# Five small early writes on the store queue, spaced by Pool fills, ahead of a split SiLU-and-multiply kernel

## The chip, the cores and the metric

The kernel runs on one core of one Trainium2 chip. The metric is device time in microseconds (us), the median of several executions. The kernel does no TensorE work. ACT (ScalarE) and DVE (VectorE) compute, Pool (GpSimd) fills, and SP (SyncE) issues DMAs; L74 is line 74 of the kernel.

## The reference, cut to what matters

```python
batch, seq, dim = (32, 512, 2048)          # x, float32
half_dim = x.shape[-1] // 2
x1, x2 = x[..., :half_dim], x[..., half_dim:]
silu_x1 = x1 * (1 / (1 + np.exp(-x1)))
return (silu_x1 * x2).astype(np.float32)   # (32, 512, 1024)
```

The input has 134.22 MB and the output 67.11 MB. There is little arithmetic per byte.

## The kernel before

The 16384 rows are cut into 16 tiles of 128 partitions x 8 rows. Loads are issued from ACT's queue and stores from SP's queue. Two input buffers and two output buffers rotate.

```python
    in_pool = ctx.enter_context(tc.tile_pool(name="in_pool", bufs=2))
    out_pool = ctx.enter_context(tc.tile_pool(name="out_pool", bufs=2))
    # ... cut ...
    def load(i):
        xt = in_pool.tile([P, K, in_cols], dt, name="xt")
        nc.scalar.dma_start(out=xt[:, :plan[i][1], :], in_=view(x_flat, i))
        loaded[i] = xt

    load(0)
    load(1)
    for i in range(n_tiles):
        # ... cut ...
        ot = out_pool.tile([P, K, half], dt, name="ot")
        for c in range(0, k, KC):                      # KC = 2: four pieces
            # ... cut: ACT writes silu into ot, DVE multiplies ot by the other half of xt ...
            if last:
                nc.sync.dma_start(out=ov[:, c:ce, :], in_=ot[:, c:ce, :])
        if not last:
            nc.sync.dma_start(out=ov, in_=ot[:, :k, :])
        if i + 2 < n_tiles:
            load(i + 2)
```

Load i+2 is issued only when tile i has been multiplied, because it reuses that tile's input buffer. Tile i can start only when the output buffer of tile i-2 has been stored.

Of the kernel before, what the change touches and what calls it, by code (L numbers as in the profile page):

```python
# [1 line left out]

# [4 lines left out]


def issue_ahead_of_the_first_barrier(nc):




    head, body = nc.main_func.blocks[:2]
    load = next(ins for ins in body.instructions if type(ins).__name__ == "InstDMACopy")
    at = next(
        j for j, ins in enumerate(head.instructions)
        if ins.engine == load.engine and type(ins).__name__ == "InstDrain"
    )
    body.instructions = [ins for ins in body.instructions if ins.name != load.name]  # L20
    head.instructions = head.instructions[:at] + [load] + head.instructions[at:]


@with_exitstack
def kernel(
    ctx: ExitStack,
    tc: tile.TileContext,
    x: bass.AP,
    out: bass.AP,
):  # L30






    nc = tc.nc
    P = nc.NUM_PARTITIONS

    x_flat = x.flatten_outer_dims()  # L40
    out_flat = out.flatten_outer_dims()
    num_rows, in_cols = x_flat.shape
    half = in_cols // 2
    dt = x_flat.dtype

    K = 8
    KC = 2
    PLAN = [K] * (num_rows // (P * K))

    in_pool = ctx.enter_context(tc.tile_pool(name="in_pool", bufs=2))  # L50
    out_pool = ctx.enter_context(tc.tile_pool(name="out_pool", bufs=2))

    plan = []
    row = 0
    for k in PLAN:
        plan.append((row, k))
        row += P * k
    assert row == num_rows
    n_tiles = len(plan)

    def view(flat, i):
        row0, k = plan[i]
        return flat[row0:row0 + P * k].rearrange("(p k) d -> p k d", k=k)

    nc.at_finalize(issue_ahead_of_the_first_barrier)


    ctx.enter_context(tc.manual_schedule())

    loaded = {}  # L70
# [5 lines that stand above are left out]

    load(0)
    load(1)
    for i in range(n_tiles):
        k = plan[i][1]  # L80
        xt = loaded.pop(i)
        last = i == n_tiles - 1
        ov = view(out_flat, i)
        ot = out_pool.tile([P, K, half], dt, name="ot")
        for c in range(0, k, KC):
            ce = min(c + KC, k)
            nc.scalar.activation(  # L87
                out=ot[:, c:ce, :],
                in_=xt[:, c:ce, :half],
                func=mybir.ActivationFunctionType.Silu,  # L90
            )
            nc.vector.tensor_mul(  # L92
                out=ot[:, c:ce, :],
                in0=ot[:, c:ce, :],
                in1=xt[:, c:ce, half:],
# [9 lines that stand above are left out]
# [1 line left out]
_INS = ['x']  # L106
_OUTS = [((32, 512, 1024), 'float32')]


# [23 lines left out]
```

## Time and profile before

| | before |
|---|---|
| time, median of 3 runs | 471.02 us (470.53 to 471.09) |
| span of the profiled run | 468.9 us |
| DVE, ACT busy | 30%, 25% |
| load and store packets, share of 16 DMA engines | 66.4% + 33.2% |

Lines of the page of the kernel before: the span, the busy times, the row of slices for DMA (each digit is the busy share of one fortieth of the span, 9 meaning 90% or more), and the two DMA queues with packets, MB and share of 16 engines' span. Queue 10 carries the loads, queue 1 the stores.

```profile
span 468.9 us, 269 instructions
DVE 142.3 (30%) x64; ACT 118.2 (25%) x65; POOL 0.2 (0%) x4
DMA  9899999999999998999999999999999989999998
...
q10 hardware_dynamic: 2304, 134.22, 66.4%
q1 hardware_dynamic: 2736, 67.11, 33.2%
...
out_dram<-ot SPq DMA_DIRECT2D x15, 4096.0 KB, 39.8
```

The two shares add up to 99.6%: the sixteen DMA engines are the limit, from start to end. The other engines wait for data. Any change of the time must show up as DMA work that was added, or as time in which the DMA engines had nothing to do.

The timeline of the kernel before, around the first store (start, duration, engine and line, operation; in brackets the idle time of the engine before it and what ended it):

```profile
32.74 81.08 SPq L100 DMA_DIRECT2D out_dram<-ot  x4
32.75 0.35 ACTq L74 DMA_DIRECT2D xt<-in_x_dram  x1
44.54 7.31 ACT L87 ACTIVATE ot<-xt 128x2048 f32<-128x2048 f32 x4 [15.36 <-DMA xt<-in_x_dram]
46.48 8.89 DVE L92 TENSOR_TENSOR ot<-ot,xt 128x2048 f32<-128x2048 f32 x4 [13.77 <-ACT ot L87]
55.41 0.37 ACTq L74 DMA_DIRECT2D xt<-in_x_dram  x1
```

Store 0 and load 2 are issued at 32.74 us, tile 1 starts at 44.54 us, when its data has landed, and load 3 is issued at 55.41 us. (The SPq line joins the first four stores; only its start is used.)

The trace also has every DMA packet. A load packet is the eight rows of one partition, 64 KB, and takes 2.418 us; a store packet is 32 KB and takes 1.213 us. Here is one engine around the first store of the kernel before, worked out from those records (start in us, L for load or S for store, duration in ns). The records do not name the engine: a packet is put behind the one that ends where it starts. Each DMA also ends, on each engine, with a semaphore packet of 4 bytes (9 ns), which reports its completion; these are left out here:

```
33.27 L 2441   35.72 L 3380   39.09 S 1213   40.30 L 2418   42.71 S 1213   43.91 S 1213   45.10 L 2418
```

On every engine the last load packet before the first store packet is long. The mean excess over 2.42 us is 0.87 us. After that, loads and stores follow each other without a gap and at full speed. The first load packets of the run are long too, by 0.6 us. An intent to make the store queue "warm" can only aim at this 0.87 us, which is 0.2% of the time.

### The profile page before, as it was taken

The page shows a single profiled execution, that of the slowest core. Times are in us where ns is not written, and L with a number is a line of the kernel's source. Part 1 is how long each engine was busy: PE and PEld are TensorE (multiplying, and loading weights), DVE is VectorE, ACT ScalarE, POOL GpSimd, SP SyncE. Part 2 cuts the span into 40 slices and gives each one's busy share as a digit, 9 for nine tenths or more (in the row PEclk, how much of TensorE's full clock was granted, in tenths as well). Part 3 has the DMA queues.
Part 4 walks back from the last instruction along what each step waited for, and adds up shares of the span by engine and source line. Part 5 has one row for each costly group of instructions (what it writes and reads, how often), then busy time and mean ns, then how long its engine had stood idle before and what let it go on. Part 6 is the DMA issues. An engine that isn't in the chain of part 4 may idle for free.

```text
span 468.9 us, 269 instructions
## 1 busy us (share of the span) xinstructions
DVE 142.3 (30%) x64; ACT 118.2 (25%) x65; POOL 0.2 (0%) x4
## 2 busy tenths in 40 slices
DVE  0070705106061160601507025070250702407034
ACT  1142406023060330603206032060420604106051
POOL 0000000000000000000000000000000000000000
DMA  9899999999999998999999999999999989999998
GB/s 431 375 447 403 447 447 447 403 419 431 447 447 403 447 492 363 442 492 391 458 403 439 456 447 403 409 442 447 447 403 444 467 386 447 442 419 481 400 409 354
DMA packets 5042, 201.35 MB, mean 429 GB/s; under 512 B 560, under 2 KB 560, under 8 KB 560
## 3 DMA queue, kind: packets, MB, share of 16 engines
q10 hardware_dynamic: 2304, 134.22, 66.4%
q1 hardware_dynamic: 2736, 67.11, 33.2%
q14 instruction: 2, 0.02, 0.0%
HBM read 134.22 MB, written 67.11 MB: 429 GB/s over the span
## 4 chain that ended last, share of the span: by engine, by line
DMA 80%; DVE 15%; ACT 3%; DVEq 0%; issue 0%
DMA xt<-in_x_dram 80%; DVE ot L92 15%; ACT ot L87 3%; DVEq L128 0%
## 5 line engine op out<-in xcount | busy, mean ns | idle before, releaser
L92 DVE TENSOR_TENSOR ot<-ot,xt 128x2048 f32<-128x2048 f32 x64 | 142.3, 2286 | 319.5 <-ACT ot L87 319.5
L87 ACT ACTIVATE ot<-xt 128x2048 f32<-128x2048 f32 x64 | 116.9, 1897 | 338.8 <-DMA xt<-in_x_dram 338.8
L87 ACT ACT_TABLE_LOAD x1 | 1.3, 1283 | 1.3 <-PEq L117 1.3
L117 POOL MEMSET const-uint8-127<- 128x1 uint8 x1 | 0.1, 102 | 0.0
L117 POOL MEMSET const-bfloat16-1.0<- 128x1 bf16 x1 | 0.1, 101 | 0.0
L117 POOL MEMSET const-float32-0.0<- 128x1 f32 x1 | 0.1, 98 | 0.2 <-issue 0.2
L117 POOL MEMSET const-float32-1.0<- 128x1 f32 x1 | 0.1, 98 | 0.0
## 6 DMA issues: line engine op xcount, KB each, us to landing
out_dram<-ot SPq DMA_DIRECT2D x15, 4096.0 KB, 39.8
out_dram<-ot SPq DMA_DIRECT2D x4, 1024.0 KB, 5.7
xt<-in_x_dram ACTq DMA_DIRECT2D x16, 47.1
```

Of the source, the lines that this page charges most:

```text
L87: nc.scalar.activation(out=ot[:, c:ce, :], in_=xt[:, c:ce, :half], func=mybir.ActivationFunctionType.Silu,)
L92: nc.vector.tensor_mul(out=ot[:, c:ce, :], in0=ot[:, c:ce, :], in1=xt[:, c:ce, half:],)
L117: nc = _bacc.Bacc("TRN2", target_bir_lowering=False, num_devices=1)
```

## The change

The intent, as its form suggests, is to let the store queue do a few tiny writes while the first two loads run, so that its first real store does not pay a start-up cost. Each write sends 512 bytes from each of 16 partitions, one packet per DMA engine, to places that the store of tile 0 overwrites. A Pool fill between the writes spaces them.

```diff
     K = 8
     KC = 2
+    WARM = 5
 ...
     load(0)
     load(1)
+    wt = out_pool.tile([P, K, half], dt, name="ot")
+    for _ in range(WARM):
+        nc.gpsimd.memset(wt[:, :4, :], 0.0)
+        nc.sync.dma_start(out=view(out_flat, 0)[:16, 0, :128], in_=wt[:16, 0, :128])
```

Each fill must wait for the write before it, which reads the tile. The writes stand ahead of store 0 on SP, and store 0 overwrites their bytes. The tile is one of the two output buffers, so tile 1 cannot start before the last small write has landed.

## The prediction

> **What bounds the kernel.** DMA, nearly without a gap. In the page's table of DMA queues the load queue's packets take 66.4% and the store queue's 33.2% of 16 engines' span; in the rows of slices DMA is at 9 throughout, DVE 30%, ACT 25%. In the trace's DMA packets a 64 KB load packet takes 2.418 us, a 32 KB store packet 1.213 us. One engine carries 128 of each: 464.8 of the 468.9 us span. The rest is 1.1 us before the first packet, 0.6 us by which the first load packets are long, 0.87 us per engine by which the last load packet before the first store packet is long (about 3.3 us, starting near 36 us), and 1.2 us after the last. The chain of waits puts 80% on the loads' DMA; its DVE and ACT pieces (15%, 3%) run while DMA is full.
>
> **What the change does.**
> 1. Removes nothing. If the 0.87 us is a cold cost of the store queue (the only candidate for a gain, 0.2%), the first small write now meets it, on engines equally saturated by loads: moved to about 8 us, not saved.
> 2. Adds 5 x 16 writes of 512 B. From the 8 KB store packets at the end (0.309 us, about 7 ns over the size's share) I estimate 0.03 us each, 0.15 us per engine. If instead every empty-to-busy switch of the store queue costs 0.87 us, five cost 4.4 us; I give that one chance in five.
> 3. Adds five Pool fills of 128x4096 f32; the trace has none such. The Trainium skill, "GPSIMD Engine Reference", section "Performance versus the Vector engine", gives 1.03 cycles per element at 1.2 GHz for port-bound bodies: estimate 3.5 us; no run here shows it yet. Pool is idle, so this costs nothing itself.
> 4. Delays. Each fill must wait until the write before it has read the tile. The Trainium skill, "DMA: Bandwidth & Descriptors", section "Queues, rings and completion order", says each DMA engine round-robins between queues by packets; the trace agrees (store 0, issued at 32.7 us, gets its first packet at 38.9, behind two load packets, then the queues alternate). So a write needs 5 to 6.5 us, a round 8.5 to 10 us, and the five end at 42 to 52 us. Store 0, behind them on SP, is issued then instead of at 32.7. The extra tile takes an output buffer, so tile 1's ACT may wait for it, and load 3, issued at 55.4 now, for that.
>
> **How much is critical.** Almost none of the delays: loads 1 and 2 fill the engines until about 61 us even without a store. They land earlier, store 0 later; the bytes are the same. At the end tile 15's arithmetic has about 3 us of slack, and more stores queued late only add to it. Only rounds over about 14 us (fill over 8 us) would empty the DMA queues and cost 10 us or more.
>
> **Prediction.** 471.02 + 0.15 (packets) + 0.2 (interleaving): 471.4 us, range 470.5 to 474.0. Faster by over 2%: 0.01; within 2%: 0.93; slower by over 2%: 0.06.
>
> **What would show it.** DMA at 9 in all slices after 2 us; the long load packets before the first small write instead of near 36 us; store 0 issued at 42 to 52 us; load 1 landing near 42 instead of 44.5 us; Pool about 17 us busy; small writes landing in 5 to 7 us.
>
> **What would make it wrong.** Rounds over 14 us; a switch cost paid by every small write (+4 us); or a saving, if the cold cost is hidden when a small write pays it.

## The result, and the profile after

The changed kernel took 471.95 us (median of 4 runs, 471.81 to 472.52), against 471.0 us (4 runs). The ratio is 1.0024, with a 95% interval of 1.0007 to 1.0042. Ratios are the mean time of one kernel's fast runs over that of the other's of the same rounds, so they are not quite the ratio of the medians quoted. The change makes the kernel slower by about one microsecond; within the margin of 2% it counts as the same.

Lines of the page of the changed kernel that answer to those of before, with the group of the fills (busy us, mean ns, then idle time before them) and the issues of the small writes (KB each, median us from issue to landing):

```profile
span 470.2 us, 293 instructions
DVE 142.4 (30%) x64; ACT 118.2 (25%) x65; POOL 17.8 (4%) x9
DMA  9999999999999999999999999999999999999988
...
q10 hardware_dynamic: 2304, 134.22, 66.2%
q1 hardware_dynamic: 2896, 67.15, 33.4%
...
L86 POOL MEMSET ot<- 128x4096 f32 x5 | 17.6, 3511 | 32.0 <-DMA out_dram<-ot 31.5
...
out_dram<-ot SPq DMA_DIRECT2D x15, 4096.0 KB, 46.9
out_dram<-ot SPq DMA_DIRECT2D x5, 8.0 KB, 8.3
```

A fill takes 3.51 us, but a write of 8 KB takes 8.3 us. So a round takes about 12 us. DVE is no slower for the fills (142.4 against 142.3 us), although little of its work runs beside one here; in e2_late_one below the whole first tile does, and DVE needs the same 8.90 us for it.

The timeline of the changed kernel:

```profile
4.47 45.89 SPq L87 DMA_DIRECT2D out_dram<-ot  x5
12.55 3.51 POOL L86 MEMSET ot<- 128x4096 f32 x1 [8.11 <-DMA out_dram<-ot]
22.46 3.51 POOL L86 MEMSET ot<- 128x4096 f32 x1 [6.40 <-DMA out_dram<-ot]
33.07 0.34 ACTq L75 DMA_DIRECT2D xt<-in_x_dram  x1
34.39 3.51 POOL L86 MEMSET ot<- 128x4096 f32 x1 [8.42 <-DMA out_dram<-ot]
46.51 3.51 POOL L86 MEMSET ot<- 128x4096 f32 x1 [8.60 <-DMA out_dram<-ot]
58.55 54.37 SPq L110 DMA_DIRECT2D out_dram<-ot  x4
58.58 7.31 ACT L97 ACTIVATE ot<-xt 128x2048 f32<-128x2048 f32 x4 [29.07 <-DMA out_dram<-ot]
69.45 0.36 ACTq L75 DMA_DIRECT2D xt<-in_x_dram  x1
71.39 7.31 ACT L97 ACTIVATE ot<-xt 128x2048 f32<-128x2048 f32 x4 [5.50 <-DMA out_dram<-ot]
```

The five writes end at 58.5 us, long after load 1 landed (41.5 us, by its semaphores). Store 0 is issued at 58.55 us instead of 32.74. Tile 1 starts at 58.58 us, held by a small write ("<-DMA out_dram<-ot"), not by its data. So load 3 is issued at 69.45 us instead of 55.41.

The wait of ACT for output buffers, which did not exist before, has its own line in the view of waits of the changed kernel (us in total, times, longest):

```profile
ACT ot L97 <- DMA xt<-in_x_dram: 303.4, 14, 23.0
ACT ot L97 <- DMA out_dram<-ot: 34.6, 2, 29.1
```

Such a wait by an engine with spare time costs nothing as long as the DMA engines have work. They nearly run out. The stretch from 58 to 76 us in the view by windows (window, its length, busy us of DVE, ACT and POOL, clock, DMA share, GB/s), first of the kernel before, then of the changed one:

```profile
58.00:76.00 18.00, 0.53 (x1) 2.47 (x2) 0.00 (x0) 1.00 1.01 437
```

```profile
58.00:76.00 18.00, 11.57 (x6) 11.92 (x7) 0.00 (x0) 1.00 0.93 353
```

(A packet is counted where it starts, so a share can exceed 1.) One engine of the changed kernel in that stretch, from the packet records as above:

```
55.26 L 2418   57.68 L 2419   60.10 S 1516   61.62 S 1213   ... five more ...   68.87 S 1213
70.41 S 1928   72.32 L 3065   75.40 S 1213   76.61 L 2418
```

Load 2's last packet ends at 60.1 us. Store 0 then runs alone. It is done at 70.1 us; the next store and load 3, issued at 69.45 us, start a little too late, and both start with long packets.

The sum closes. From the packet records, per engine:

| | before | after |
|---|---|---|
| packets at their usual length | 465.27 us | 465.45 us |
| long first load packets | 0.63 | 0.67 |
| long packets at the first large store | 0.87 (36 us) | 0.57 (60 us) |
| long packets of the restart | none | 1.37 (70 to 75 us) |
| standing still near 70 us | none | 0.11 |

The five writes are 5 x (27 + 9) ns = 0.18 us, the second term being the semaphore packet. The other rows add 0.04 - 0.30 + 1.37 + 0.11 = 1.22 us. Together that is 1.40 us. The last DMA packet ends 1.39 us later than before (469.02 against 467.63 us), and the span grew by 1.3 us.

### The profile page after: what moved, and what is told of

It is laid out like the page before. It is cut to its first block, busy times and chain, and to the rows that moved or that the text cites. A ratio compares the mean times of both kernels' runs of the same rounds, so it can differ in the third digit from the quotient of the medians.

```text
span 470.2 us, 293 instructions
## 1 busy us (share of the span) xinstructions
DVE 142.4 (30%) x64; ACT 118.2 (25%) x65; POOL 17.8 (4%) x9
## 4 chain that ended last, share of the span: by engine, by line
DMA 75%; DVE 15%; ACT 3%; POOL 3%; POOLq 1%; DVEq 0%; issue 0%; ACTq 0%
DMA xt<-in_x_dram 67%; DVE ot L102 15%; DMA out_dram<-ot 8%; ACT ot L97 3%; POOL ot L86 3%; POOLq L138 1%; DVEq L138 0%; POOLq L86 0%; ACTq L97 0%; POOLq L127 0%
## 5 line engine op out<-in xcount | busy, mean ns | idle before, releaser
L102 DVE TENSOR_TENSOR ot<-ot,xt 128x2048 f32<-128x2048 f32 x64 | 142.4, 2287 | 318.7 <-ACT ot L97 318.7
L86 POOL MEMSET ot<- 128x4096 f32 x5 | 17.6, 3511 | 32.0 <-DMA out_dram<-ot 31.5
```

The costliest lines, as they stand in the source:

```text
L86: nc.gpsimd.memset(wt[:, :4, :], 0.0)
L102: nc.vector.tensor_mul(out=ot[:, c:ce, :], in0=ot[:, c:ce, :], in1=xt[:, c:ce, half:],)
```

## The experiments

Theory A: the microsecond comes from the delay of store 0 and tile 1, which lets the DMA queues run dry for a moment and restart. Theory B: it comes from the small writes and fills themselves. A second question is whether small writes take away the 0.87 us at the first store. Twelve kernels ran; the times are medians (of e11_half_packets and e12_half_alone with their slow runs, which the ratios leave out; they are called slow by their time alone, the clock was 1.0 in all), and "before" is the kernel before in the same rounds. The "extra" column is the length of the DMA activity in the profiled run over the sum of its packets at their usual length, worked out from the packet records (1.22 us in the kernel before, 2.44 in the changed one).

| run | edit | time | before | ratio (95%) | extra us |
|---|---|---|---|---|---|
| e1_two | two rounds | 470.85 | 470.81 | 1.0000 (0.9987 to 1.0012) | 1.25 |
| e2_late_one | 14 fills, one write | 472.08 | 470.81 | 1.0023 (1.0010 to 1.0035) | 2.47 |
| e3_packed | one fill, five writes | 471.14 | 470.81 | 1.0003 (0.9989 to 1.0016) | 1.28 |
| e4_three | three rounds | 471.10 | 470.81 | 1.0001 (0.9989 to 1.0014) | 1.46 |
| e5_four | four rounds | 470.85 | 470.89 | 0.9999 (0.9987 to 1.0012) | 1.31 |
| e6_six | six rounds | 476.92 | 470.89 | 1.0127 (1.0112 to 1.0143) | 7.29 |
| e7_own_buffer | writes from a third tile | 475.50 | 470.89 | 1.0097 (1.0083 to 1.0110) | 5.93 |
| e8_hold | 18 fills, no write | 478.64 | 470.89 | 1.0163 (1.0149 to 1.0177) | 9.12 |
| e9_large_first | one early 32 KB write per engine | 473.65 | 471.00 | 1.0060 (1.0048 to 1.0072) | 2.77 |
| e10_hold_short | 15 fills, no write | 471.04 | 471.00 | 1.0002 (0.9989 to 1.0015) | 1.44 |
| e11_half_packets | changed kernel, loads halved | 477.40 | 471.00 | 1.0138 (1.0105 to 1.0171) | 4.20 |
| e12_half_alone | kernel before, loads halved | 490.53 | 470.79 | 1.0318 (1.0297 to 1.0340) | 16.07 |

### Fewer rounds: two, three, four

```diff
-    WARM = 5
+    WARM = 2        # e1_two;  3 in e4_three,  4 in e5_four
```

> The loop runs twice instead of five times, so both small writes should have landed by about 22.4 us (as the second did in the changed kernel), before store 0 is ready at 32.7 us: nothing is delayed. Theory A (the changed kernel lost its time because store 0 and tile 1 were held until 58.5 us, so that the DMA queues drained at 60 and 70 us and restarted with long packets): no loss, the time is within 0.3 us of before or below it. Theory B (each small write or fill costs time itself, 1.0 us over five): about 0.4 us slower than before. On the long load packets near 36 us in the kernel before (0.87 us per engine): if they are a cost that the store queue pays once and a small write hides, they are gone and the time is about 0.7 us below before, 470.3; if they belong to the first large store, they are back and the time is that of before, 471.0 to 471.1.

> Three rounds: the third write should land near 34.3 us as in the changed kernel, so store 0 is held by about 1.5 us only and tile 1 not at all (its data lands near 42 us). Theory A: no loss, the same time as with two, within 0.2 us. Theory B: about 0.6 us over before.

> Four rounds: the fourth write lands near 46.4 us, so store 0 is issued 13.7 us late and tile 1 starts about 5 us after its data. Load 3 is then issued near 57.3 us, before load 2's last packet (60 us). Theory A (only a drained DMA queue costs): no loss, 470.8 to 471.1, no long packets after the ones before the first store packet. If instead every us by which store 0 is held costs a little (1.0 us for the 26 us of the changed kernel), 0.5 us over before.

None of the three differs from before. The timeline of e5_four:

```profile
46.42 101.42 SPq L110 DMA_DIRECT2D out_dram<-ot  x5
46.54 7.31 ACT L97 ACTIVATE ot<-xt 128x2048 f32<-128x2048 f32 x4 [17.06 <-DMA out_dram<-ot]
57.41 0.36 ACTq L75 DMA_DIRECT2D xt<-in_x_dram  x1
```

With four rounds store 0 waits until 46.42 us and tile 1 until 46.54 us, and nothing is lost: as long as load 3 is issued before the work already queued (load 2 and store 0) runs out, the engines have work. So the cost is not one per write, and not one in proportion to the delay. It comes with the fifth round only.

The 0.87 us did not go away. In e1_two the load packets ahead of store 0 are long by 0.90 us, in e4_three by 1.08 us (there a small write had landed 34.2 us into the run, just before store 0), in e5_four by 0.82 us, when store 0 comes at 46 us. No packet was long at the first small write near 9 us in any of them. Small writes neither pay this cost nor remove it. The expectation for the case "a small write hides it", 470.3 us, failed.

### One late write

```diff
-    for _ in range(WARM):
-        nc.gpsimd.memset(wt[:, :4, :], 0.0)
-        nc.sync.dma_start(out=view(out_flat, 0)[:16, 0, :128], in_=wt[:16, 0, :128])
+    for _ in range(14):
+        nc.gpsimd.memset(wt[:, :4, :], 0.0)
+    nc.sync.dma_start(out=view(out_flat, 0)[:16, 0, :128], in_=wt[:16, 0, :128])
```

> Fourteen fills in a row, then one small write: it should be issued near 50 us and land near 58.5 us as the fifth of the changed kernel did, so store 0 and tile 1 are held as long, with four writes fewer. Theory A: the same loss as the changed kernel, 471.9 to 472.1, with long packets near 60 and 70 to 72 us. Theory B (cost per write): about 0.2 us over before, 471.2. If the fills are what costs: 14 of them against 5, about 2.5 us over before.

It came out at 472.08 us, the loss of the changed kernel, with one write in place of five and nearly three times the fills. Its timeline has the same times:

```profile
0.94 49.90 POOL L86 MEMSET ot<- 128x4096 f32 x14 [0.50 <-POOLq L127]
50.87 0.37 SPq L87 DMA_DIRECT2D out_dram<-ot  x1
58.49 24.23 SPq L110 DMA_DIRECT2D out_dram<-ot  x3
58.52 7.31 ACT L97 ACTIVATE ot<-xt 128x2048 f32<-128x2048 f32 x4 [29.04 <-DMA out_dram<-ot]
69.39 0.37 ACTq L75 DMA_DIRECT2D xt<-in_x_dram  x1
```

The long packets are there too: 0.71 us near 60 us and 1.23 us near 70 us. This is the clearest run for theory A against theory B.

### Five writes without the delay

The edit against the kernel before; the tile `wt` is taken from `out_pool` as in the changed kernel.

```diff
+    nc.gpsimd.memset(wt[:, :4, :], 0.0)
+    for j in range(WARM):
+        cols = slice(128 * j, 128 * (j + 1))
+        nc.sync.dma_start(out=view(out_flat, 0)[:16, 0, cols], in_=wt[:16, 0, cols])
```

> One fill, then five small writes at once, to five different columns (none waits for another): all five should have landed by about 13 to 22 us, so nothing is delayed. Theory A: no loss, within 0.3 us of before or below it, as with two spaced writes. Theory B: as slow as the changed kernel, about 1 us over before. The long packets near 36 us come out as in the run with two spaced writes; if they do not, the spacing matters.

All five writes are kept and nothing is held; store 0 is issued at 33.07 us:

```profile
33.07 52.14 SPq L111 DMA_DIRECT2D out_dram<-ot  x3
```

The time is that of before. The writes landed later than I expected, the last at 29.3 us, still in time. Their packets, from the records, show why a small write is so slow beside large loads (earliest of 16 engines, us):

```
data      8.95   13.80   18.66   21.11   25.97
semaphore 11.38  16.24   21.10   23.55   28.41
```

After its data packet, each write's semaphore packet waits 2.44 us, one load packet, and the next write's data waits one more. (The third and fourth write are closer: the load queue was then going from load 0 to load 1.) In the changed kernel it is the same: issued at 4.47 us, data from 9.02 us, semaphore packet from 11.46 us, landed at 12.43 us. The second write of the changed kernel fell on that change from load 0 to load 1, and its semaphore followed its data by 0.03 us; its round was 2 us shorter (6.40 us of waiting in the timeline, against 8.11 to 8.60). The Trainium skill, "DMA: Bandwidth & Descriptors", section "Queues, rings and completion order", says that an engine round-robins between queues packet by packet; the records agree, and add that the completion of a small write takes a turn of its own.

### One more round

```diff
-    WARM = 5
+    WARM = 6
```

> Six rounds: the sixth fill runs from 58.6 to 62.1 us, and its write, on a load queue that ended at 60.2 us, lands near 64.3 us. Theory A: the engines stand still from 60.2 to about 65.2 us, run store 0 alone (9.7 us), then stand still again for about 1 us until load 3, issued near 75.2 us: 6 us of standstill in place of about 0.3, so 476 to 478 us, 1.1 to 1.5% over before. Theory B (cost per write and fill): 0.2 us more than the changed kernel, 472.2.

476.92 us, as theory A had it. The row of DMA slices shows the hole, in the sixth slice (59.4 to 71.3 us):

```profile
DMA  9999969999999999999999999999999999999988
```

An engine's records have nothing but the 36 ns of the sixth write between 60.0 and 64.3 us and nothing between 74.05 and 75.14 us, 5.4 us in all. (That write, on idle engines, landed 1.33 us after its issue; the median beside the loads was 8.3 us.) The restart adds long packets of 1.46 us; the 0.87 us is absent, as store 0 started on idle engines with a first packet of 1.214 us. So 5.4 + 1.46 - 0.87 = 6.0 us, which is what was lost. The fifth round stands at the edge of a cliff: the sixth costs about five times as much as the first five together (476.92 - 471.95 against 0.95 us).

### The two delays apart

The small writes hold two things, store 0 on SP and an output buffer. First, only store 0:

```diff
+    warm_pool = ctx.enter_context(tc.tile_pool(name="warm_pool", bufs=1))
-    wt = out_pool.tile([P, K, half], dt, name="ot")
+    wt = warm_pool.tile([P, 2, half], dt, name="wt")
     for _ in range(WARM):
-        nc.gpsimd.memset(wt[:, :4, :], 0.0)
+        nc.gpsimd.memset(wt[:, :2, :], 0.0)
+        nc.gpsimd.memset(wt[:, :2, :], 0.0)
```

> Five rounds, but the writes come from a tile of their own (8 KB per partition, filled twice per round), so tile 1 gets its output buffer at once and load 3 is issued near 53 us; store 0 is still held to 58.5 us. This tells the two delays apart. If the drain at 70 us came from tile 1 waiting for the buffer of the small writes, the long packets at 60 and 70 us are gone. But tile 2 needs the output buffer of tile 0, whose store now alternates with load 3 and lands near 89 us; load 4 is then issued near 100 us, where load 3 ended near 89 and store 1 near 99: a new drain of about 1 us near 100 us, and 471.5 to 472.5 us. If the held store 0 costs nothing by itself: 470.9.

The place was right and the size was not: 475.5 us. Giving the writes a buffer of their own makes the kernel slower than the changed one. Its timeline:

```profile
52.31 0.33 ACTq L76 DMA_DIRECT2D xt<-in_x_dram  x1
58.44 86.88 SPq L112 DMA_DIRECT2D out_dram<-ot  x5
91.08 7.31 ACT L99 ACTIVATE ot<-xt 128x2048 f32<-128x2048 f32 x4 [42.33 <-DMA out_dram<-ot]
101.94 0.36 ACTq L76 DMA_DIRECT2D xt<-in_x_dram  x1
```

Load 3 is issued early, at 52.31 us, so the late store 0 has to share the engines with it and lands only at about 91 us. Tile 2 needs that output buffer. Load 4 is issued at 101.94 us, and an engine's records show nothing from 99.57 to 102.92 us (the longest gap of the sixteen engines; the mean is 2.9 us), followed by long packets of 1.45 us. I had estimated a hole of 1 us. In the changed kernel, tile 1's own delay left store 0 alone on the engines, so that it was stored by 71.4 us: one delay softened the other.

Then only the buffer, with fills and no write at all:

```diff
-    for _ in range(WARM):
-        nc.gpsimd.memset(wt[:, :4, :], 0.0)
-        nc.sync.dma_start(out=view(out_flat, 0)[:16, 0, :128], in_=wt[:16, 0, :128])
+    for _ in range(18):        # e8_hold;  15 in e10_hold_short
+        nc.gpsimd.memset(wt[:, :4, :], 0.0)
```

> Eighteen fills and no write at all: the output buffer is held until about 65.1 us, store 0 is issued at 32.9 us as before. Only tile 1 is late: done at 76.0 us, when load 3 and store 1 are issued. The engines have work until about 70.3 us (three loads and one store: 3 x 19.34 + 9.70 + the 1.5 us of long packets + 1.1). Theory A: a standstill from 70.3 to about 76.9 us and a restart with long packets of 0.6 to 1.4 us: 477.5 to 479 us. If held buffers alone cost nothing: 471.

> Fifteen fills and no write: the output buffer is held until about 54.4 us instead of 65.2 us, so tile 1 is done near 65.4 us and load 3 is issued there, before the engines run out of loads at 70.3 us. Theory A: a delay of 10 us for tile 1 and load 3 costs nothing, 470.7 to 471.1 us. A cost in proportion to the delay (7.8 us for 20 us of delay in the run with eighteen fills) would be about 3.9 us: 474.8.

The view by timeline of e8_hold, then of e10_hold_short:

```profile
65.16 7.31 ACT L96 ACTIVATE ot<-xt 128x2048 f32<-128x2048 f32 x4 [35.82 <-POOL ot L86]
76.03 0.37 ACTq L75 DMA_DIRECT2D xt<-in_x_dram  x1
```

```profile
54.43 7.31 ACT L96 ACTIVATE ot<-xt 128x2048 f32<-128x2048 f32 x4 [25.09 <-POOL ot L86]
65.31 0.37 ACTq L75 DMA_DIRECT2D xt<-in_x_dram  x1
```

With 15 fills load 3 is 10 us late and the time is that of before, 471.04 us. With 18 fills it is 20.6 us late and the time is 478.64 us. The limit lies between, at about 70 us, when the work already queued ends. In e8_hold an engine stands still from 70.55 to 76.98 us (the mean of the sixteen is 6.2 us) and restarts with long packets of 1.46 us: 6.2 + 1.5 = 7.7 us, against 7.75 us lost. Fifteen fills, 53 us of Pool work beside everything else, cost nothing by themselves.

### A large early write

```diff
-    for _ in range(WARM):
-        nc.gpsimd.memset(wt[:, :4, :], 0.0)
-        nc.sync.dma_start(out=view(out_flat, 0)[:16, 0, :128], in_=wt[:16, 0, :128])
+    for c in (0, 4):
+        nc.gpsimd.memset(wt[:, c:c + 4, :], 0.0)
+    nc.sync.dma_start(out=view(out_flat, 0)[:16], in_=wt[:16])
```

> Two fills, then one early write of 32 KB per engine (sixteen rows of tile 0's first eight, the size of a store packet), issued near 8 us and landed by about 18 us: nothing is delayed. Its bytes cost 1.2 us. What it tells: the 0.87 us of long load packets. If the first large packet of the store queue pays it once, the long packets move to about 10 us and are gone near 36 us: 470.85 + 1.2 = 472.1 us. If it comes each time the store queue starts beside running loads, it is at both places: 472.9 us. If the early write pays nothing and store 0 still does, it belongs to store 0's own shape: 472.1 us with the long packets near 36 us only.

Here the store packets near 11 us are long, by 2.34 us on average, and the load packets ahead of store 0 are not long any more. The time is 473.65 us. The sum is 1.21 us of bytes, plus 2.34, minus 0.87, which is 2.68 us; 2.65 us was measured. So a first large packet does pay the cost in place of store 0, as the first of the three expectations said, but it paid 2.34 us and not 0.87. Nothing is to be had from it. Why it costs more there was not settled.

### Smaller load packets, a test that did not work

```diff
-        nc.scalar.dma_start(out=xt[:, :plan[i][1], :], in_=view(x_flat, i))
+        for c in (0, K // 2):
+            nc.scalar.dma_start(out=xt[:, c:c + K // 2, :], in_=view(x_flat, i)[:, c:c + K // 2, :])
```

> The changed kernel with each load issued as two of 32 KB per partition, so that load packets take 1.21 us instead of 2.42. In the changed kernel a small write waited behind two load packets, and its semaphore packet behind a third, 8 us in all. If that is what sets its time, it lands in 4.5 to 5.5 us here, a round takes 8 to 9 us, the fifth write lands near 41 to 45 us, store 0 is held only 9 to 12 us, nothing drains and the loss is gone: 470.7 to 471.4 us with all five writes and fills in place. If the small writes have a fixed latency near 8 us whatever is queued, rounds stay at 12 us and the time at 472.

> The kernel before, with each load issued as two of 32 KB per partition, and no small writes or fills: the control for the last run, which came out at 474.9 to 493.7 us although its small writes took only 6.1 us. If halving the loads is what scattered that run, this one is as slow and scattered, 474 to 480 us, and the last run says nothing of the small writes' cost. If the small writes were the cause there, this one is at 471 us.

The small writes became faster, with a median of 6.1 us in place of 8.3, and rounds of about 10 us. The first one's semaphore packet came 1.23 us after its data instead of 2.44: the turn shrank with the load packet. The wait before the data shrank less: on the first engine to start, the data came 3.4 to 4.1 us after the issue, against 4.6 to 5.1 us in the changed kernel, with load packets half as long. So the wait before the data is not a fixed number of load packets; what else is in it was not settled. The time says nothing about the small writes: halving the loads in the kernel before made it 490.53 us by itself (484.1 to 486.8 us in the three fast runs, 494 to 501 us in three slow ones), and the run with small writes scattered from 474.9 to 481.2 us, with one slow run at 493.65. The records of e12_half_alone show where its time went: from 466.3 to 478.5 us never more than one of the sixteen engines has a packet. One engine had fallen behind the others: the semaphore packets of the last half load lie 23.8 us apart, against 0.8 us for the last load of the kernel before. Why the engines drift apart with halved loads was not tested, nor why the run with small writes came out faster than its control (they ran on different chips).

No experiment pointed to a version that beats both kernels.

## Why the prediction was right or wrong

- **Time and direction: right, in part by luck.** 471.95 us lies in the range 470.5 to 474.0, and "within 2%" was given 0.93. The figure in the middle was low, though: +0.4 us forecast, +0.95 measured, and the difference is a drain that the prediction placed at rounds of 14 us. That the drain at 12 us cost one microsecond is luck: with one round more (e6_six) the time is 476.92 us. The reason, that the DMA engines are full from start to end, holds: the packets fill 99.6% of the span in both kernels, and the two variants that shift work by about 10 us or more without draining the queues (e5_four, e10_hold_short) take the time of before.
- **Packets of the writes, "0.15 us per engine": right.** 0.18 us measured.
- **Fills, "estimate 3.5 us" from the 1.03 cycles per element at 1.2 GHz of the Trainium skill's "GPSIMD Engine Reference", section "Performance versus the Vector engine": right.** 3.51 us measured for 4096 elements per partition; Pool was busy for 17.8 us.
- **"So a write needs 5 to 6.5 us, a round 8.5 to 10 us, and the five end at 42 to 52 us": wrong in size.** A write took 8.3 us, a round 12 us, and the five ended at 58.5 us. The term left out is the turn of the semaphore packet, 2.44 us behind another load packet (four of the five writes had it).
- **"Only rounds over about 14 us (fill over 8 us) would empty the DMA queues and cost 10 us or more": wrong, the slack was over-stated.** At 12 us the queues already ran dry for 0.11 us. I compared the end of the writes with the end of load 2 (about 61 us), and even by that five rounds of 12 us are at the limit. The event that counts is the issue of load 3, 10.9 us after tile 1 starts, against the end of store 0 at 70.1 us. The runs with five, six and eighteen put that limit near 70 us.
- **"0.2 (interleaving)": mis-sized.** What stood in its place was 1.22 us of long packets and standing still at 60 and 70 us. This is the loss that the forecast of 471.4 lacks.
- **The 0.87 us "moved to about 8 us, not saved": half wrong.** It was not saved, but it did not move to the first small write. It stayed with the first large store, at 60 us in the changed kernel (0.57 us there), and in e1_two, e3_packed, e4_three and e5_four at its full size. Only a large early write took it over.
- **The one chance in five that each small write pays a switch cost:** it did not come. No packet of the changed kernel was long at the first small write, and beside the later ones the excess was 0.02 us at most.
- **"More stores queued late only add to" the slack at the end: right.** The last DVE multiplication of the changed kernel ends at 461.0 us and the DMA works on to 469.0 us.

## What to carry to other kernels

When one resource is full from start to end, work moved to another place costs nothing until that resource runs dry. Find the instruction whose lateness empties its queue, here the issue of load 3, and work out the slack to that moment, not to the end of the transfer beside it. A tiny DMA beside large packets is not cheap in latency (8.3 us here), as its data and its completion each wait their turn; do not put it ahead of a large store on the same queue, or in a buffer that the main loop needs. A warm-up of a queue with writes of another size than the real ones warmed nothing here.

## What the Trainium skill lacked or had wrong

- "DMA: Bandwidth & Descriptors", "Queues, rings and completion order": it states the round robin between queues by packets of several descriptors, but not that the semaphore packet of a small write takes a turn of its own. Measured: 2.44 us between data and semaphore packet beside 64 KB load packets, 1.23 us beside 32 KB ones; 4.86 us from one small write's data to the next. Beside these loads a turn was one 64 KB packet of the trace's records; how many descriptors that is, the trace does not show.
- The same page, "Anatomy of one DMA — SWDGE (gpsimd) path", gives a fixed cost of about 2 us per DMA, for the path from GpSimd: here 8 KB issued from SP beside running loads took a median of 8.3 us to land, and 1.33 us when the engines were idle (the sixth write of e6_six). No page gives the time to landing of a small DMA beside running loads.
- No page has the long packets at the first large store of a run: 0.87 us per engine beside running loads, not removed by one to five earlier writes of 512 bytes, taken over (at 2.34 us) by one early write of 32 KB per engine. After both queues had run dry, the first store and load packets were long by about 0.7 us each; but a first large store that started alone on idle engines was not long (first packet 1.214 us, e6_six). What sets these is open.
- Agreement, for completeness: the 1.03 cycles per element of "GPSIMD Engine Reference" fits the fill of 3.51 us, and the ceiling of 435 GB/s of "DMA: Bandwidth & Descriptors", section "Where 436 GB/s comes from", fits 433 GB/s over the steady part of the kernel before (108 to 440 us), although that section expects about 358 GB/s to bind for transfers between HBM and SBUF; this kernel, on one core, was not held to that.
